# Moving three sets of instructions in a two-layer encoder kernel: third weight sums, differential values, last neighbourhood heads

## The chip, the cores and the metric

The kernel runs on one core of one Trainium2 chip. The metric is the device time of one execution in microseconds; lower is better. The core has engines that each work through their own queue in order: TensorE (PE in the profile; PEld is its weight load), VectorE (DVE), ScalarE (ACT), GpSimd (POOL) and SyncE (SP, which here only issues DMAs). They wait for each other by semaphores.

## The reference

An encoder trunk of two layers over 512 tokens of width 1024, in float32. In each layer three mixers read the same normalised input: differential attention (4 heads of two 64-wide query and key pairs, value width 128), a gated convolution of 31 taps over 512 channels, and neighbourhood attention (8 heads of 64 on a grid of 8 by 64 positions, window 8 by 16, with a bias table per head). Their projections are merged by sigmoid gates, go through an output matrix, then a SwiGLU feed-forward part of width 2816 and a gated per-layer input. A last norm ends it.

```
proj = h @ w_in[i]
qa, ka, va, glu_in, qc, kc, vc, gates = jnp.split(proj, SPLITS, axis=-1)
ya = diff_attention(qa, ka, va, ...)
yb = conformer_conv(glu_in, ...)
yc = neighbourhood_attention(qc, kc, vc, rpb[i])
merged = ga * (ya @ w_br_a[i]) + gb * (yb @ w_br_b[i]) + gc * (yc @ w_br_c[i])
x = x + merged @ w_o[i]
h = rmsnorm(x, norm_ffn[i])
x = x + (jax.nn.silu(h @ w_ffn_gate[i]) * (h @ w_ffn_up[i])) @ w_ffn_down[i]
```

## The kernel before

Channels lie on the 128 partitions and the 512 tokens run along the free axis. Every float32 number that enters a matmul is split into a high half (a ScalarE copy to fp32r) and a low half (a VectorE subtraction, source minus high half), and each product is made of three matmuls: high by high, high by low, low by high (`split`, line 157; `mm3`, lines 177 to 179). So each weight block costs a DMA on SyncE's queue (`weights`, line 171), a copy on ScalarE and a subtraction on VectorE before TensorE can use it. Buffers rotate: 3 for raw weights (`wr`), 3 each for their halves (`wh`, `wl`), 2 for `r` and `kh`, 3 `mm` accumulators in PSUM, 2 `sc`, 2 `tr`, 1 `av`.

TensorE's order is the order of the program text. The other engines are ordered by a scheduler from priorities; weights get a head start (`high_priority`). `behind(i, then)` adds an order between two instructions of the same queue without a semaphore.

Attention units are woven into the projections. `later(gen, delay, gap)` queues a unit; `chunk()` counts blocks of matmuls, every fourth is a tick (`tick`), and at a tick the next due unit emits its next step. In `natten_in(pr, ...)` (phase natten, pr 0 to 3, two heads each) the queries and keys of a pair of heads are projected and split, DMAs stack them (`stack`), and four units (half of the tokens by head, called unit 0 to 3 here) are queued with a delay of 10 ticks for pr 0 and 5 for the others. A unit (`natten_unit`) loads its bias block (`natten_b`, line 675), makes scores (`natten_sc`, line 784), reads them out on VectorE with the bias (line 683), makes exponentials on ScalarE (`natten_e`), takes reciprocals (line 695) and scales; two ticks later TensorE transposes the result (`natten_tr`, lines 707 to 711), it is split (`natten_pt`, `natten_a`); two ticks later it is multiplied by the values (`natten_av` or `natten_mm`, lines 726, 727). The units of pr 3 run while `diff_in(0)`, `diff_v(0)` and `diff_in(1)` project the differential attention.

`diff_v` calls `values` (lines 575 to 603): 512 tokens by 256 value channels in two accumulators of a `mm` buffer each, `accs[0]` for token tiles 0 and 1 and `accs[1]` for 2 and 3. For each of the 8 chunks k of the contraction it does token tiles t = 0 to 3 in turn, three matmuls each (lines 588, 590, 592), with `chunk()` called twice per k. Weights come in two blocks, k = 0 to 3 and k = 4 to 7.

After the mixers, `merge_b` writes the 8 merged chunks (`mergeb_y`, `mergeb_v`: ScalarE copy, VectorE low half), and `w_o` multiplies them by the output matrix, row block after row block, adds the residual, makes the operand of the feed-forward part (`wo_h`) and its sum of squares (`wo_ss`), whose norm follows (`wo_tr`, `wo_sm`, POOL's `wo_rc`, and `wo_tr` again). Along the way `quarters` (lines 911 to 938) makes four combinations of 256-token quarters for each pair of chunks, and splits each: `wo_rp`, `wo_e`, `wo_z`.

The feed-forward part works in 22 blocks fb. Block 0 is done plainly. For all others `seven` (lines 940 to 1018) computes gate and up products of a block by seven products instead of eight, from sums of weight quarters: s1 and s2 are built by loading a block and accumulating another onto it by a DMA from POOL's queue (`ffn_qk<-w_fu`, line 955); s3 = s1 + a22 and s4 = s3 + a12 are two VectorE additions (`ffn_qk<-ffn_qk,ffn_r` and `ffn_qk<-ffn_qk,ffn_wr`), where a22 is a block loaded into an `r` buffer (`ffn_r<-w_fu`, line 953) and a12 is the second half of the block's gate weights. s3 and s4 are then split into `ffn_pt` (odd fb) or `ffn_y` (even fb). TensorE uses them in the sixth and seventh product. The addition s3 is put behind the low half of a22 and, where `first` is set (fb 8, 9, 15 and 16), behind `self.held`, the last low half of an earlier operand.

Of the kernel before, what the change touches and what calls it, by code (L numbers as in the profile page):

```python
# [20 lines left out]
P = 128  # L21
# [5 lines left out]
KD = 8  # L27
# [34 lines left out]
class Net:  # L62
# [512 lines left out]
    def values(self, ap, parts):  # L575


        mm = self.nc.tensor.matmul
        accs = [self.ps("mm", (P, 2, 256)) for _ in range(2)]
        for o in range(0, KD, 4):  # L580
            wh, wl = self.weights(ap[:, o * 256:(o + 4) * 256], 1024)
            for k in range(o, o + 4):
                s = slice((k - o) * 256, (k - o + 1) * 256)
                for t in range(4):
                    out = accs[t // 2][:, t % 2, :]
                    ts = slice(t * P, (t + 1) * P)

                    mm(out, self.h[k][:, 0, ts], wh[:, s], start=k == 0 and t % 2 == 0,
                       stop=False, skip_group_check=True)
                    mm(out, self.h[k][:, 0, ts], wl[:, s], start=False, stop=False,  # L590
                       skip_group_check=True)
                    mm(out, self.h[k][:, 1, ts], wh[:, s], start=False,
                       stop=k == KD - 1 and t % 2 == 1, skip_group_check=True)
                self.chunk()
                self.chunk()
        vs = []
        for acc in accs:
            v = self.sb("v", [P, 2, 512], F32R)
            for t in range(2):
                for hi, lo, a in parts(v[:, t], acc[:, t]):  # L600
                    self.split(hi, lo, a)
            vs.append(v)
        return vs

    def natten_in(self, pr, st, ys):

        self.phase = "natten"
        st4 = self.sb("qk", [P, 4, 512], F32R)
        k2 = self.sb("x", [P, 2, 512], F32R)
        for s, off in enumerate((OFF_QC, OFF_KC)):  # L610
            ps = self.proj(off + pr * P)
            f = 1.0 if s else 0.125
            nat, low = self.sb("kh", [P, 512], F32R), self.sb("t", [P, 512], F32R)
            if pr == 0:

                t = low.bitcast(F32)
                self.stt(t, ps, f, self.rb, ALU.mult, ALU.mult)
                ps, f = t, 1.0
            self.act(nat, ps, AF.Copy, scale=f)
            self.background(self.stt(low, ps, f, nat.bitcast(F32), ALU.mult, ALU.subtract),  # L620
                            self.bg["natten"])
            self.stack(nat, low, st4[:, 2 * s:2 * s + 2], k2 if s else None)
        ys.append(self.sb("y", [P, 2, 512], F32R))
        for n in range(4):
            self.later(self.natten_unit(pr, n // 2, n % 2, st4, k2, st, ys[pr]), 5 if pr else 10, 1)

    def stack(self, nat, low, one, two):

# [282 lines left out]
    def quarters(self, x, h, j):  # L911


        one, two = slice(0, 256), slice(256, 512)
        g = lambda k: self.par(self.i, "ffn", k)
        f = []
        for k in (2 * j, 2 * j + 1):
            v = self.sb("t", [P, 512])
            self.act(v, x[k], AF.Copy, scale=g(k))
            f.append(v)  # L920
        b11, b12, b21, b22 = f[0][:, one], f[0][:, two], f[1][:, one], f[1][:, two]
        u = self.sb("t", [P, 2, 256])
        w = self.sb("t", [P, 2, 256])
        t1, t2, t3, t4 = u[:, 0], u[:, 1], w[:, 0], w[:, 1]
        self.tt(t1, b11, b12, ALU.subtract)
        self.tt(t2, b22, t1, ALU.add)
        self.tt(t3, b22, b12, ALU.subtract)
        self.tt(t4, t2, b21, ALU.subtract)
        if j < 2:
            d = [self.sb("rp" if n < 2 else "e", [P, 2, 256], F32R) for n in range(4)]  # L930
        else:
            d = [q for n in range(2) for q in self.zs[2 * j - 4 + n]]
        for o, t in zip(d, (t1, t2, t3, t4)):
            self.split(o[:, 0], o[:, 1], t)
        ha, hb = self.halves(h[2 * j]), self.halves(h[2 * j + 1])
        cut = lambda p, c: (p[0][:, c], p[1][:, c])
        return dict(b11=cut(ha, one), b21=cut(hb, one), b22=cut(hb, two),
                    **{f"t{n + 1}": (o[:, 0], o[:, 1]) for n, o in enumerate(d)})

    def seven(self, wg, wu, bs, tags, spare, md, first):  # L940


        nc = self.nc
        with self.tc.high_priority(offset=min(self.w_ahead, self.tc.cur_priority - self.p0)):
            lo, up = slice(0, 512), slice(512, 1024)
            g, a22 = self.sb("wr", [P, 1024]), self.sb("r", [P, 512])
            sums = self.sums[self.sevens % 3], self.sums[3]
            self.sevens += 1
            s1, s2, s3, s4 = (s[:, q:q + 512] for s in sums for q in (0, 512))
            nc.sync.dma_start(s1, wg[:, lo])  # L950
            nc.sync.dma_start(s2, wu[:, up])
            nc.sync.dma_start(g, wg)
            nc.sync.dma_start(a22, wu[:, up])
            for q in (s1, s2):
                nc.gpsimd.dma_start(q, wu[:, lo], accum_op=ALU.add)  # L955
            ws = {}

            def halve(hi, lo, src, names):
                i = self.split(hi, lo, src)
                for q, name in enumerate(names):  # L960
                    c = slice(q * 512, q * 512 + 512)
                    ws[name] = (hi[:, c], lo[:, c])
                return i

            wide = lambda: (self.sb("wh", [P, 1024], F32R), self.sb("wl", [P, 1024], F32R))
            halve(*wide(), g, ("a11", "a12"))
            low = halve(self.sb("kh", [P, 512], F32R), self.sb("a", [P, 512], F32R), a22, ("a22",))
            halve(*wide(), sums[0], ("s1", "s2"))
            i = self.tt(s3, s1, a22, ALU.add)
            self.behind(i, low)  # L970
            if first:
                self.behind(i, self.held)
            self.tt(s4, s3, g[:, up], ALU.add)
            halve(*spare, sums[1], ("s3", "s4"))
# [13 lines left out]
        o = self.sb("t", [P, 2, 256])  # L988
# [50 lines left out]
    def ffn(self, h, x):  # L1039
# [7 lines left out]
        for part in PARTS:  # L1047
            mids = []
            for f, fb in enumerate(part):
                tags = (("mm", "mm", "mm"), ("sc", "sc", "av"))[fb % 2]  # L1050
                md = md8[f]
                mids.append(md)
                wg, wu = self.a["w_fg"][i, fb], self.a["w_fu"][i, fb]
                if fb:
                    self.seven(wg, wu, bs, tags, spare[fb % 2], md, part[0] and f < 2)
                    continue
                g = self.sb("t", [P, 512])
                pg, pu = (self.ps(t) for t in tags[:2])
                for j in range(len(QUARTERS), 4):
                    self.four.append(self.quarters(x, h, j))  # L1060
                self.pair((pg, pu), (wg, wu), [h[k] for k in ORDER])

                def gate(pg=pg, g=g):
                    self.tt(g, pg, self.rb, ALU.mult)
                    self.act(g, g, AF.Silu, table="silu")

                self.ready(gate)

                def up(pu=pu, g=g, md=md):
                    self.tt(g, g, pu, ALU.mult)  # L1070
                    self.split(md[:, 0, :], md[:, 1, :], g)

                self.ready(up)
            self.flush()
            down = [self.a["w_fd"][i, m][:, part[0] * P:(part[-1] + 1) * P] for m in range(KD)]
            two = [self.ps(("mm", "sc")[fb % 2 == 0]) for _ in range(2)]
            self.pair(two, down[:2], mids)
            for m in range(KD):
                if m < 2:
                    ps = two[m]  # L1080
                else:
                    ps = self.ps("mm")
                    self.gemm(ps, down[m], mids)
                d = self.sb("t", [P, 512])
                self.tt(d, ps, self.rb, ALU.mult)
                self.tt(x[m], x[m], d, ALU.add)
                if part is PARTS[-1]:
                    if m in (0, 2):
                        qk = self.parts_of("qk", [2, 512], 2, F32R)
                    hn.append(self.norm_chunk(m, x[m], self.par(i, "ple", m),  # L1090
                                              qk[m % 2] if m < 4 else "z", st))
# [315 lines left out]
```

## Time and profile before

| what | value |
|---|---|
| median of 3 runs | 1793.07 us (1792.29 to 1793.09) |
| the profiled execution's own time | 1792.81 us |
| its span from the first to the last instruction | 1791.0 us |
| mean granted TensorE clock | 0.998 |
| PE busy | 1774.5 us (99%) |
| DVE busy | 1410.6 us (79%) |
| ACT busy | 891.6 us (50%) |
| POOL busy | 99.3 us (6%) |
| mean DMA rate | 142 GB/s |

In the rows, a timeline line gives the start in us from the span's start, the duration, engine, source line, operation, output<-inputs by the program's names, shape and count, and in square brackets the idle time of that engine before it and what ended it. A row of waits gives engine, tile and line that waited, whom it waited for, the total in us, how often, and the longest. A row of windows gives a stretch, its length, the busy time of each engine in it with the number of instructions, the granted TensorE clock (1.00 is full), and the DMA share and rate. The whole program is two layers, so a stretch of the first layer comes back 886.9 us later in the second.

### The profile page before, as it was taken

The numbers are of one execution on the slowest core, as the hardware profiler recorded it, in microseconds if no ns is written. First come the engines' busy times: TensorE is split into PE (matmuls) and PEld (weight loads), VectorE is DVE, ScalarE is ACT, GpSimd is POOL, SyncE is SP. The second block draws the span as 40 slices with busy tenths as digits, with TensorE's granted clock in tenths as the row PEclk, the third lists the DMA queues.
The fourth block names the chain that finished last, engine by engine and source line by source line (L and its number), as shares of the span: only waits on it lengthen the run. The fifth ranks groups of instructions, "written<-read, shape, count | busy, mean of one in ns | idle before, by whom it ended". The sixth has DMA issues, their size and how long they took to land.

```text
span 1791.0 us, 27255 instructions
## 1 busy us (share of the span) xinstructions
PE 1774.5 (99%) x10138; PEld 1559.7 (87%) x10138; DVE 1410.6 (79%) x2394; ACT 891.6 (50%) x1551; POOL 99.3 (6%) x142
## 2 busy tenths in 40 slices
PE   9999999999999999999999999999999999999998
PEld 7888888888799899998888888888887998989987
DVE  7877888997788587787776788889887885877776
ACT  5577555325565254454535765552355652534444
POOL 0000000000111011100000000000001110101000
PEclk9999999999999999999999999999999999999999
DMA  5665541334747365544447655422356563746332
GB/s 206 190 182 169 159 124 46 108 98 150 217 130 188 111 166 154 140 123 127 145 125 200 170 161 148 112 71 95 97 182 186 153 173 108 182 133 159 98 103 94
DMA packets 112212, 254.48 MB, mean 142 GB/s; under 512 B 14416, under 2 KB 19024, under 8 KB 112080
## 3 DMA queue, kind: packets, MB, share of 16 engines
q1 hardware_dynamic: 99264, 229.40, 41.9%
q0 software_dynamic: 12096, 22.03, 7.8%
q8 instruction: 80, 1.31, 0.3%
q10 hardware_dynamic: 720, 1.31, 0.2%
q14 instruction: 52, 0.43, 0.1%
HBM read 213.89 MB, written 7.34 MB: 124 GB/s over the span
## 4 chain that ended last, share of the span: by engine, by line
PE 91%; DVE 4%; DMA 2%; ACT 2%; issue 1%; SPq 0%; DVEq 0%; POOLq 0%; ACTq 0%
PE ffn_mm L177 5%; PE ffn_mm L178 5%; PE ffn_mm L179 5%; PE ffn_mm L985 4%; PE ffn_mm L984 4%; PE ffn_mm L983 4%; PE ffn_sc L985 3%; PE ffn_sc L984 3%; PE ffn_sc L983 3%; PE mergea_mm L178 2%; PE mergea_mm L179 2%; PE mergea_mm L177 2%; PE diff_sc L784 2%; PE gatec_mm L177 2%; PE gatec_mm L178 2%; PE gatec_mm L179 2%
## 5 line engine op out<-in xcount | busy, mean ns | idle before, releaser
L160 DVE SCALAR_TENSOR_TENSOR conv_z<-glu_z,pre_par,conv_z 128x512 f32<-128x512 f32 x240 | 179.6, 748 | 3.3
L143 ACT ACTIVATE ffn_wh<-ffn_wr 128x1024 fp32r<-128x1024 f32 (+1 forms) x94 | 94.9, 1015 | 110.0 <-PE ffn_mm L178 75.1
L157 DVE TENSOR_TENSOR ffn_wl<-ffn_wr,ffn_wh 128x1024 fp32r<-128x1024 f32 (+1 forms) x94 | 109.9, 1174 | 5.1 <-ACT ffn_wh L143 4.6
L955 POOL DMA_DIRECT2D ffn_qk<-w_fu x84 | 74.6, 996 | 550.5 <-DMA ffn_qk<-w_fu 218.1
L157 DVE TENSOR_TENSOR ffn_t<-ffn_mm,wo_rb 128x512 f32<-128x512 f32 (+1 forms) x66 | 40.0, 607 | 68.3 <-PE ffn_mm L179 68.3
L143 ACT ACTIVATE mergea_wh<-mergea_wr 128x1024 fp32r<-128x1024 f32 (+1 forms) x32 | 27.1, 846 | 96.8 <-PE mergea_mm L178 79.5
L177 PE MATMUL ffn_mm<-ffn_v,ffn_wh 128*128 128x512 f32 x176 | 68.5, 389 | 0.0
L178 PE MATMUL ffn_mm<-ffn_v,ffn_wh 128*128 128x512 f32 x176 | 68.5, 389 | 0.0
L179 PE MATMUL ffn_mm<-ffn_v,ffn_wl 128*128 128x512 f32 x176 | 68.5, 389 | 0.0
L157 DVE TENSOR_TENSOR ffn_wl<-ffn_qk,ffn_wh 128x1024 fp32r<-128x1024 f32 x42 | 51.4, 1225 | 19.9 <-ACT ffn_wh L143 19.9
L143 ACT ACTIVATE ffn_wh<-ffn_qk 128x1024 fp32r<-128x1024 f32 x42 | 44.5, 1060 | 43.7 <-PE ffn_mm L178 24.5
L157 DVE TENSOR_TENSOR ffn_t<-ffn_t,ffn_t 128x512 f32<-128x512 f32 (+1 forms) x48 | 31.4, 659 | 32.1 <-ACT ffn_t L143 31.5
L143 ACT ACTIVATE diff_a<-diff_sc,diff_s 128x512 f32<-128x512 f32 x32 | 22.0, 687 | 59.0 <-DVE diff_s L875 59.0
L983 PE MATMUL ffn_sc<-wo_h,ffn_wh 128*128 128x256 f32 x176 | 50.0, 284 | 0.0
L985 PE MATMUL ffn_sc<-wo_h,ffn_wl 128*128 128x256 f32 x176 | 49.8, 283 | 0.0
L984 PE MATMUL ffn_sc<-wo_h,ffn_wh 128*128 128x256 f32 x176 | 49.8, 283 | 0.0
L143 ACT ACTIVATE natten_wh<-natten_wr 128x1024 fp32r<-128x1024 f32 x24 | 25.4, 1058 | 41.4 <-issue 15.2
L984 PE MATMUL ffn_mm<-wo_h,ffn_wh 128*128 128x256 f32 x160 | 45.3, 283 | 0.0
L985 PE MATMUL ffn_mm<-wo_h,ffn_wl 128*128 128x256 f32 x160 | 45.3, 283 | 0.0
L983 PE MATMUL ffn_mm<-wo_h,ffn_wh 128*128 128x256 f32 x160 | 45.3, 283 | 0.0
L875 DVE TENSOR_REDUCE diff_s<-diff_sc 128x1 f32<-128x512 f32 x64 | 42.0, 684 | 3.5 <-PE diff_sc L784 3.4
L143 ACT ACTIVATE ffn_kh<-ffn_r 128x512 fp32r<-128x512 f32 x42 | 26.6, 632 | 32.8 <-PE ffn_mm L984 16.2
(825 smaller groups left out, 6577.0 us busy)
## 6 DMA issues: line engine op xcount, KB each, us to landing
ffn_wr<-w_fg SPq DMA_DIRECT2D x44, 512.0 KB, 3.9
ffn_qk<-w_fu POOLq DMA_DIRECT2D x84, 256.0 KB, 5.5
ffn_wr<-w_fd SPq DMA_DIRECT2D x32, 448.0 KB, 3.8
ffn_r<-w_fu SPq DMA_DIRECT2D x42, 256.0 KB, 4.8
ffn_qk<-w_fg SPq DMA_DIRECT2D x42, 256.0 KB, 3.9
ffn_qk<-w_fu SPq DMA_DIRECT2D x42, 256.0 KB, 4.2
natten_wr<-w_in SPq DMA_DIRECT2D x16, 512.0 KB, 4.1
natten_b<-bias SPq DMA_DIRECT2D x32, 256.0 KB, 3.8
```

Of the source, the lines that this page charges most:

```text
L143: i = self.nc.scalar.activation(out, in_, func, **kw)
L157: return self.nc.vector.tensor_tensor(out, a, b, op)
L160: return self.nc.vector.scalar_tensor_tensor(out, a, s, b, op0, op1)
L177: mm(out, wh, ah, start=first, stop=False)
L178: mm(out, wh, al, start=False, stop=False)
L179: mm(out, wl, ah, start=False, stop=last)
L784: self.nc.tensor.matmul(out, st4[:, u, qs], st[:, ks], start=n == 0, stop=n == 1)
L875: nc.vector.tensor_reduce(out=m[:, u:u + 1], in_=sc, op=ALU.max, axis=AX.X, negate=True)
L955: nc.gpsimd.dma_start(q, wu[:, lo], accum_op=ALU.add)
L983: mm(out, wh[:, c], bh, start=first and k == 0, stop=False, skip_group_check=True)
L984: mm(out, wh[:, c], bl, start=False, stop=False, skip_group_check=True)
L985: mm(out, wl[:, c], bh, start=False, stop=k == 3, skip_group_check=True)
```

## The change

Three edits. In `values`, for the first weight block only, the 16 pairs of chunk and token tile are sorted so that all those of `accs[0]` come before those of `accs[1]`; `chunk()` is called after every second pair, as often as before. In `natten_in`, the units of the last pair of heads (pr 3) get a delay of 6 ticks instead of 5. In `quarters`, each split is remembered in `self.held`, and in `seven` the addition s3 of fb 1 and fb 2 is put behind it too.

```diff
@@ values
-            for k in range(o, o + 4):
+            both = [(k, t) for k in range(o, o + 4) for t in range(4)]
+            if o == 0:
+                both.sort(key=lambda kt: kt[1] // 2)
+            for n, (k, t) in enumerate(both):
                 s = slice((k - o) * 256, (k - o + 1) * 256)
-                for t in range(4):
-                    out = accs[t // 2][:, t % 2, :]
...
-                self.chunk()
-                self.chunk()
+                out = accs[t // 2][:, t % 2, :]
...
+                if n % 2:
+                    self.chunk()
@@ natten_in
-            self.later(self.natten_unit(pr, n // 2, n % 2, st4, k2, st, ys[pr]), 5 if pr else 10, 1)
+            self.later(self.natten_unit(pr, n // 2, n % 2, st4, k2, st, ys[pr]), 6 if pr == 3 else 5 if pr else 10, 1)
@@ quarters
         for o, t in zip(d, (t1, t2, t3, t4)):
-            self.split(o[:, 0], o[:, 1], t)
+            self.held = self.split(o[:, 0], o[:, 1], t)
@@ seven
-    def seven(self, wg, wu, bs, tags, spare, md, first):
+    def seven(self, wg, wu, bs, tags, spare, md, first, fb):
...
             i = self.tt(s3, s1, a22, ALU.add)
             self.behind(i, low)
-            if first:
+            if first or fb < 3:
                 self.behind(i, self.held)
@@ ffn
-                    self.seven(wg, wu, bs, tags, spare[fb % 2], md, part[0] and f < 2)
+                    self.seven(wg, wu, bs, tags, spare[fb % 2], md, part[0] and f < 2, fb)
```

What the built programs show: no engine has an instruction more or less. On VectorE, s3 and s4 of fb 1 and the low half of `ffn_pt` move from before the last merged chunk's low half (s3) and from the third set of quarters (s4, `ffn_pt`) to behind the last quarter's low half, where the norm's reduction stands between s3 and s4. On ScalarE the copy of `ffn_pt` moves with them. On SyncE the load of a22 for fb 3, which reuses the `r` buffer that fb 1's s3 reads, moves from between two `wo_x` loads to behind the gate weights of fb 3. fb 2's sums stand where they stood. In the neighbourhood part unit 0 to 3's scores of pr 3 come one tick later on TensorE, and SyncE issues unit 3's bias load behind the eight DMAs that stack the keys of differential head 0, instead of ahead of them. The first accumulation into `accs[1]` comes 18 matmuls later.

More of the change, by code (lines that the diff above doesn't have):

```diff
@@ L581, in values @@
             wh, wl = self.weights(ap[:, o * 256:(o + 4) * 256], 1024)
-            for k in range(o, o + 4):
+            both = [(k, t) for k in range(o, o + 4) for t in range(4)]
+            if o == 0:
+                both.sort(key=lambda kt: kt[1] // 2)
+            for n, (k, t) in enumerate(both):
                 s = slice((k - o) * 256, (k - o + 1) * 256)
-                for t in range(4):
-                    out = accs[t // 2][:, t % 2, :]
[L586 to L593, printed above, removed]
-                self.chunk()
-                self.chunk()
+                out = accs[t // 2][:, t % 2, :]
+                ts = slice(t * P, (t + 1) * P)
+                mm(out, self.h[k][:, 0, ts], wh[:, s], start=k == 0 and t % 2 == 0,
+                   stop=False, skip_group_check=True)
+                mm(out, self.h[k][:, 0, ts], wl[:, s], start=False, stop=False,
+                   skip_group_check=True)
+                mm(out, self.h[k][:, 1, ts], wh[:, s], start=False,
+                   stop=k == KD - 1 and t % 2 == 1, skip_group_check=True)
+                if n % 2:
+                    self.chunk()
         vs = []
```

## The prediction

> **What bounds the kernel now.** I read the page first: TensorE is busy for nearly the whole span, so only its idle time can be won, and each edit is worth what it takes out of TensorE's own waits.
>
> ```profile
> span 1791.0 us, 27255 instructions
> PE 1774.5 (99%) x10138; PEld 1559.7 (87%) x10138; DVE 1410.6 (79%) x2394; ACT 891.6 (50%) x1551; POOL 99.3 (6%) x142
> ```
>
> Idle is 1791.0 - 1774.5 = 16.5 us. The view of TensorE's waits says where:
>
> ```profile
> PE wo_mm L178 <- DVE mergeb_v L157: 6.0, 2, 3.6
> PE natten_tr L709 <- ACT natten_e L143: 0.8, 2, 0.4
> ```
>
> Both come twice, once per layer; the first row is met by the edit of the sums, the second by that of the neighbourhood units; a smaller wait of `diff_mm`, shown below, by that of the values. These rows undercount, since a matmul's shown end lies after the next one's start. So I price a wait by the distance of two starts, less the distance that the same instructions keep undisturbed.
>
> **Edit 1, the third sums.** The timelines of TensorE, VectorE and ScalarE in layer 0:
>
> ```profile
> 463.14 0.39 PE L179 MATMUL wo_mm<-mergeb_v,wo_wl 128*128 128x512 f32 x1
> 463.37 0.39 PE L177 MATMUL wo_mm<-mergeb_v,wo_wh 128*128 128x512 f32 x1
> 467.31 0.50 PE L178 MATMUL wo_mm<-mergeb_v,wo_wh 128*128 128x512 f32 x1 [3.56 <-DVE mergeb_v L157]
> ...
> 465.96 0.69 DVE L157 TENSOR_TENSOR ffn_qk<-ffn_qk,ffn_r 128x512 f32<-128x512 f32 x1 [8.29 <-DMA ffn_qk<-w_fu]
> 466.57 0.69 DVE L157 TENSOR_TENSOR mergeb_v<-gatec_x,mergeb_v 128x512 fp32r<-128x512 f32 x1
> ...
> 457.71 0.63 ACT L143 ACTIVATE mergeb_v<-gatec_x 128x512 fp32r<-128x512 f32 x1 [1.70 <-DVE gatec_x L157]
> ```
>
> VectorE's queue is in order. The s3 of fb 1 stands at its head for 8.29 us, waiting for an accumulating load, and behind it the last merged chunk's low half, whose high half ScalarE had at 458.34. TensorE runs dry. The change puts s3 behind the last quarter's low half; then the low half runs at about 458.4 and is done by 459.1, 4.5 us before TensorE asks (463.60). So the whole wait goes: 467.31 - 463.37 - 0.23 = 3.71 us. Layer 1 has the same wait and something more:
>
> ```profile
> 1350.15 0.39 PE L177 MATMUL wo_mm<-mergeb_v,wo_wh 128*128 128x512 f32 x1
> 1352.99 0.75 PE L178 MATMUL wo_mm<-mergeb_v,wo_wh 128*128 128x512 f32 x1 [2.46 <-DVE mergeb_v L157]
> 1356.52 0.39 PE L177 MATMUL wo_mm<-mergeb_y,wo_wh 128*128 128x512 f32 x1
> ...
> 467.31:470.72 3.41, 3.41 (x15) 2.84 (x16) 2.63 (x4) 2.82 (x4) 1.76 (x2) 1.00 0.90 176
> 1353.00:1356.50 3.50, 3.50 (x8) 2.76 (x9) 1.70 (x3) 2.44 (x3) 1.73 (x2) 0.51 1.09 233
> ```
>
> The wait is 2.84 - 0.23 = 2.61 us, but the next 8 matmuls take 3.53 us where 8 x 0.23 = 1.84 would do: 1.69 more, at a granted clock of 0.51. In layer 0 a longer wait left it at 1.00. The slow stretch goes with its wait, so layer 1 gives 4.30 and both give 8.01 us.
>
> [...]
>
> What is late next? The moved work must still be on time:
>
> ```profile
> 485.10 0.69 DVE L157 TENSOR_TENSOR wo_x<-wo_x,wo_mm 128x512 f32<-128x512 f32 x1 [1.79 <-PE wo_mm L179]
> ...
> 508.09 0.69 DVE L215 TENSOR_REDUCE wo_sm<-wo_tr 128x4 f32<-128x512 f32 x1
> ...
> 509.13 1.03 POOL L222 TENSOR_TENSOR wo_rc<-wo_sm,pre_power 128x4 f32<-128x4 f32 x1 [38.93 <-DVE wo_sm L218]
> ...
> 512.59 0.60 PE L226 MATMUL wo_tr<-pre_ident,wo_rc 128*128 128x128 f32 x4
> ...
> 520.22 0.28 PE L983 MATMUL ffn_sc<-wo_rp,ffn_pt 128*128 128x256 f32 x1
> ...
> L157 DVE TENSOR_TENSOR ffn_wl<-ffn_qk,ffn_wh 128x1024 fp32r<-128x1024 f32 x42 | 51.4, 1225 | 19.9 <-ACT ffn_wh L143 19.9
> ```
>
> VectorE caught up with TensorE at 485.10, so it follows TensorE and moves 3.7 us forward with it. The last quarter's low half ends at about 508.1 - 3.7 = 504.4. Then come, in the built order, s3, the reduction, s4 (each 0.6 from start to start, as 465.96 to 466.57): the norm gains two additions, 1.2 us. The power on POOL then ends at 510.16 - 3.7 + 1.2 = 507.7, and TensorE wants it at 512.59 - 3.7 = 508.9: 1.2 us to spare. `ffn_pt` takes 1.2 us on VectorE by the last row (same shape, 1225 ns) and, taken as long again, on ScalarE before that; s4 ends at 506.2, so it is ready at about 508.7, and wanted at 520.22 - 3.7 = 516.5. Both are hidden; the cover is the 1.2 us. VectorE also sheds s4 and the half of `ffn_pt` from its crowded middle, which I count as nothing. On SyncE the a22 load of fb 3 now waits for s3, at about 505, and the loads behind it with it; they belong to fb 3 and fb 4, which TensorE reaches two and three blocks after fb 1, so not before 516.5. `wo_x` loads, which stood behind that load, come earlier. fb 2's s3 doesn't move: nothing.
>
> **Edit 2, values tile by tile.**
>
> ```profile
> 145.47 0.28 PE L590 MATMUL diff_mm<-diff_wl,glu_h 128*128 128x256 f32 x1
> 145.59 0.28 PE L592 MATMUL diff_mm<-diff_wh,glu_h 128*128 128x256 f32 x1
> 146.16 0.39 PE L588 MATMUL diff_mm<-diff_wh,glu_h 128*128 128x256 f32 x1 [0.29 <-ACT diff_rp L143]
> ```
>
> The first matmul into `accs[1]` waits for ScalarE to empty its PSUM buffer: 0.57 - 0.12 = 0.45 us. With 18 more matmuls of 0.12 us (2.2 us) ahead of it the buffer is long free. Instruction counts stay. On ScalarE the copy of the next key weights now stands ahead of unit 0's exponentials and waits for the last use of the first value weights; the scores come at that time too, so I count nothing. Both layers: 0.90 us.
>
> **Edit 3, units a tick later.** First an undisturbed round of transposes and scores, then the disturbed one; then the same for a later unit:
>
> ```profile
> 156.18 0.28 PE L592 MATMUL diff_mm<-diff_wh,glu_h 128*128 128x256 f32 x1
> 157.32 0.28 PE L588 MATMUL diff_mm<-diff_wh,glu_h 128*128 128x256 f32 x1
> 160.07 0.28 PE L592 MATMUL diff_mm<-diff_wh,glu_h 128*128 128x256 f32 x1
> 162.53 0.40 PE L177 MATMUL diff_mm<-glu_h,diff_wh 128*128 128x512 f32 x1
> 165.80 0.29 PE L707 MATMUL natten_tr<-pre_ident,natten_e 128*128 128x128 f32 x1
> 166.28 0.48 PE L177 MATMUL diff_mm<-glu_h,diff_wh 128*128 128x512 f32 x1
> 169.63 0.29 PE L707 MATMUL natten_tr<-pre_ident,natten_e 128*128 128x128 f32 x1
> 170.56 0.47 PE L177 MATMUL diff_mm<-glu_h,diff_wh 128*128 128x512 f32 x1
> ...
> 159.53 0.16 DVE L695 RECIPROCAL natten_s<-natten_s 128x2 f32<-128x2 f32 x1
> ...
> 156.69 0.33 SPq L675 DMA_DIRECT2D natten_b<-bias  x1
> 160.30 1.14 SPq L633 DMA_DIRECT2D diff_qk<-diff_kh  x2
> 165.25 1.24 SPq L633 DMA_DIRECT2D diff_x<-diff_rp  x2
> ...
> L143 ACT ACTIVATE natten_e<-natten_b,natten_s x10: 494/500/509, 140.1 to 165.5; 128x256 f32<-128x256 f32 x10
> L683 DVE CUSTOM_DVE_ANT_0 natten_b<-natten_sc,natten_b x9: 402/423/425, 140.4 to 163.9; 128x256 f32<-128x256 f32 x9
> ...
> natten_b<-bias SPq DMA_DIRECT2D x32, 256.0 KB, 3.8
> ffn_qk<-w_fu POOLq DMA_DIRECT2D x84, 256.0 KB, 5.5
> ```
>
> Lost now: (2.46 - 1.14) + (0.93 - 0.48) = 1.77 us per layer, the first because unit 1's reciprocal sits at 159.53 behind rotary work on VectorE. One tick later the scores fall among other work: unit 1's normalised values should meet its transposes within 0.1 us. Unit 3 is the worry. Its bias load was issued at 156.69; in the built order it follows the eight stack DMAs (160.30 to 166.49 now; about 1.1 us earlier after, as unit 1's two score reads, 0.42 each, and their hand-overs move from ahead of the rotary work on VectorE to behind it). So it goes out near 165.4 and, with the median 3.8, lands at 169.2. Two score reads, exponential, reciprocal and scaling cost about 2.1 us more (0.42 twice, 0.50, 0.16, 0.50 for the like-shaped scaling, and a hand-over): 171.3. TensorE comes to unit 3's transposes at 169.63 - 0.45 - 1.32 (the waits before it) + 12 x 0.23 (one more block of matmuls) = 170.6. That is 0.7; with hand-overs I take 0.8, and 0.1 for unit 1, and so a gain of 1.77 - 0.9 = 0.87 per layer, 1.7 in both. Bounds: no wait at all gives 3.5; with the 5.5 us of POOL's 256 KB loads the waits are 2.4 + 0.1, which turns the 1.77 into a loss of 0.7, 1.4 in both. I stay near the bias load's own median. Behind unit 3's waiting read on VectorE stand unit 0's and unit 2's results, wanted later.
>
> **Sum.** 8.0 + 0.9 + 1.7 = 10.6 us off 1792.81 (the profiled execution; span 1791.0 plus 1.8 around it), which lies 0.3 below the median of the runs. On the median: 1793.07 - 10.6 = **1782.5**. What a measurement can tell from no change is about 0.2%, 3.6 us.
>
> **Rivals.**
> The half-clock stretch is not in the timed runs: 1.7 less, 1784.2. Against it, the three runs span 0.8 us (1792.29 to 1793.09) and the profiled one, which has it, lies between: 0.08.
> The late units cost as much as I bounded: 1793.07 - 8.9 + 1.4 = 1785.6. For it, the moved bias load: 0.12.
> VectorE, not TensorE, sets the pace up to the norm: its low halves still end at 508.1, the power with two additions ahead at 511.4, and TensorE, there at 508.9 (layer 1: 0.6 earlier), waits 2.5 and 3.1 us: 1782.5 + 5.6 = 1788.1. For it, VectorE's backlog at the end of this stage; against, the 1.79 us idle at 485.10: 0.12.
> The freed time is eaten up there wholly, or the order brings nothing: 1789.5 to 1796.7, taken as 1793: 0.05.
> Slower: unit 3's bias lands so late that VectorE's head blocks and TensorE idles. Each us past 169.2 costs 2 us in the two layers, and a wait over 2.5 us may add the 1.69 of half clock in each. Being 3.6 us slower needs (10.6 + 3.6 - 3.4) / 2 = 5.4 us more, a landing 9.2 us after issue; at 10 us it is 1782.5 + 12.4 + 3.4 = 1798.3. The median of 3.8 speaks against: 0.05.
>
> **Numbers.** The first case keeps 0.58; its own range is 1780.6 (no unit wait) to 1784.8 (edit 3 worth nothing, and 0.6 for a late VectorE). With the half clock and the late units that is 0.78, so the range goes up to VectorE's case: 1780.6 to 1788.1. Faster 0.58 + 0.08 + 0.12 + 0.12 = 0.90, same 0.05, slower 0.05.
>
> **What would show it.** Right: no wait of `wo_mm` for `mergeb_v`, clock 1.00 there in both layers, no wait of the first matmul into `accs[1]`, and at unit 3's transposes a wait under 1 us on `natten_e`. Wrong: TensorE waiting at the second `wo_tr` for `wo_rc`, at `ffn_pt`, or over 2 us in the neighbourhood units; or a `wo_mm` wait that stays.

## The result, and the profile after

The changed kernel takes 1783.11 us (median of 4 runs, 1782.88 to 1783.51); the kernel before, on the same chip, 1793.08 (4 runs, 1792.29 to 1794.02): a ratio of 0.9943, 95% interval 0.9927 to 0.9959. The prediction said 1782.5, in a range of 1780.6 to 1788.1. The profiled execution took 1783.16 us, 9.65 less than that of before (1792.81).

First the head of the page, then the view of TensorE's waits, all that it lists (total, times, longest):

```profile
span 1781.4 us, 27258 instructions
PE 1771.9 (99%) x10138; PEld 1558.2 (87%) x10138; DVE 1410.0 (79%) x2394; ACT 890.6 (50%) x1551; POOL 99.3 (6%) x142
```

```profile
PE pre_av L323 <- DVE pre_zeror L379: 1.1, 1, 1.1
PE natten_tr L712 <- ACT natten_e L143: 0.7, 2, 0.6
PE natten_tr L710 <- ACT natten_e L143: 0.3, 2, 0.2
PE natten_tr L712 <- DVE natten_pt L157: 0.3, 1, 0.3
PE natten_tr L712 <- DVE natten_a L157: 0.2, 1, 0.2
```

The row of `wo_mm` for `mergeb_v` (6.0 us) is gone; what is left belongs to the neighbourhood units and to the start. At the place of the sums, VectorE's timeline in layer 0, then windows of 3.4 us across the former wait in layers 0 and 1 (the columns behind the window are its length, the busy time of each engine, and behind the last brackets TensorE's granted clock, the DMA share and GB/s). In all timelines below, rows that lie between those shown are left out:

```profile
456.95 0.69 DVE L157 TENSOR_TENSOR mergeb_v<-gatec_x,mergeb_v 128x512 fp32r<-128x512 f32 x1 [0.70 <-ACT mergeb_v L143]
462.82 1.37 DVE L157 TENSOR_TENSOR wo_x<-wo_x,wo_mm 128x512 f32<-128x512 f32 x2 [5.18 <-PE wo_mm L179]
```

```profile
462.40:465.80 3.40, 3.40 (x17) 2.81 (x16) 2.98 (x4) 3.16 (x5) 0.90 (x1) 1.00 1.10 286
1345.30:1348.70 3.40, 3.40 (x16) 2.81 (x15) 2.97 (x4) 3.15 (x5) 0.88 (x1) 1.00 1.11 264
```

The low half now starts at 456.95, as soon as ScalarE has the high half, and nothing stands ahead of it. TensorE is busy through both windows, at a granted clock of 1.00.

Where the 9.65 us came from is read by laying the starts of the same TensorE instructions in the two traces side by side, at points between the edits, where the same number of instructions has been issued. The shift grows by these steps: 0.24 at the kernel's start (no edit lies there); layer 0: values 0.61, units 0.54, sums 3.85; layer 1: -0.28 at a unit of an earlier pair of heads (no edit there either), values 0.55, units -0.20, sums 4.37. The rest is within 0.05 a step.

### The profile page after: what moved, and what is told of

The parts are those of the page before. It is cut to its first block, busy times and chain, and to the rows that moved or that the text cites. A ratio compares the mean times of both kernels' runs of the same rounds, so it can differ in the third digit from the quotient of the medians.

```text
span 1781.4 us, 27258 instructions
## 1 busy us (share of the span) xinstructions
PE 1771.9 (99%) x10138; PEld 1558.2 (87%) x10138; DVE 1410.0 (79%) x2394; ACT 890.6 (50%) x1551; POOL 99.3 (6%) x142
## 4 chain that ended last, share of the span: by engine, by line
PE 95%; DVE 2%; ACT 1%; issue 1%; DMA 1%; SPq 0%; DVEq 0%; POOLq 0%; ACTq 0%
PE ffn_mm L177 5%; PE ffn_mm L178 5%; PE ffn_mm L179 5%; PE ffn_mm L988 4%; PE ffn_mm L987 4%; PE ffn_mm L986 4%; PE ffn_sc L988 3%; PE ffn_sc L987 3%; PE ffn_sc L986 3%; PE mergea_mm L177 2%; PE mergea_mm L179 2%; PE mergea_mm L178 2%; PE diff_sc L787 2%; PE gatec_mm L177 2%; PE gatec_mm L178 2%; PE gatec_mm L179 2%
```

## The experiments

The kernel before was timed again beside each group of runs, on four chips (which chip the first runs were made on isn't known here): 1795.57 us (21 runs, 1792.66 to 1797.43) beside the first four kernels, 1794.55 (9) beside the next four, 1795.23 (12) beside the three after them, 1795.11 (13) beside the last. That it is 2 us longer there than in the first runs, and scatters by 5, is a result in itself and comes up below.

**Only the sums.** The changed kernel with the loops of the values and the 5 ticks of before:

```
-            self.split(o[:, 0], o[:, 1], t)
+            self.held = self.split(o[:, 0], o[:, 1], t)
...
-            if first:
+            if first or fb < 3:
```

> Only the third sums are moved; values and units stay as before. My theory, that the parts add up and that the sums bring 3.85 us in layer 0 and 4.37 in layer 1 (the steps between the two traces): 8.2 us, about 1784.9, with no wait of wo_mm for mergeb_v in either layer and clock 1.00 there. Rival A, that the 1.7 us of half clock is a matter of the single execution: 6.4 us, about 1786.7. Rival B, that the sums bring nearly the whole difference of 10 us and the other two edits only shift waits about: about 1783.3.

1784.67 us (1784.31 to 1785.35), ratio 0.9939 (0.9926 to 0.9951). The steps are 3.87 and 4.36, no wait is left there, and the time is as expected. Against the kernel before on the same chip it is 10.9 us, more than the steps of the two first traces give: what the sums remove was larger on this chip. The two traces from it that keep the waits, those of the next two kernels, lose 9.3 and 10.8 us at them, half clock included. One step has no edit beside it: in layer 1 unit 1's transposes start 0.34 us later than in the kernel before, against the matmuls ahead of them (0.35 in the kernel with the sums in layer 0 only, below). Why is open; it blurs every step of the units in layer 1.

**Only the values.** The loops of the first chunks as changed, nothing else.

> Only the values are multiplied tile by tile in the first chunks. My theory: 0.55 us per layer, 1.1 us, about 1792.0, and the first matmul into the second accumulator pair does not wait. The 3.7 and 2.6 us waits of wo_mm stay. Rival: the earlier units meet the same late reciprocal and the wait turns up again there, 1793.1. [...]

1795.83 us (1793.13 to 1797.97), ratio 1.0002 (0.9993 to 1.0011): nothing. The wait for the accumulator pair goes and the shift there is 0.55, but 15 us later it comes back, 0.58 us of it; in layer 1, 0.55 go and 0.55 come back. TensorE, VectorE and ScalarE at unit 1, in this kernel:

```profile
160.10 0.28 PE L595 MATMUL diff_mm<-diff_wh,glu_h 128*128 128x256 f32 x1
160.14 0.16 DVE L698 RECIPROCAL natten_s<-natten_s 128x2 f32<-128x2 f32 x1
160.79 0.89 ACT L143 ACTIVATE natten_e<-natten_e,natten_s 128x256 f32<-128x256 f32 x2
161.34 0.90 PE L712 MATMUL natten_tr<-pre_ident,natten_e 128*128 128x128 f32 x4 [0.95 <-ACT natten_e L143]
```

TensorE arrives earlier at a reciprocal that is as late as ever. The rival was right.

The clock is lost at both waits of `wo_mm` here, at the one of layer 0 too: granted 0.72 in the 3.41 us from the wait's end in layer 0 (466.53) and 0.78 in as long a stretch behind them, 0.63 and 0.87 in layer 1. TensorE's timeline of layer 0 in this kernel:

```profile
463.98 0.39 PE L177 MATMUL wo_mm<-mergeb_v,wo_wh 128*128 128x512 f32 x1
466.53 0.50 PE L178 MATMUL wo_mm<-mergeb_v,wo_wh 128*128 128x512 f32 x1 [2.17 <-DVE mergeb_v L157]
...
467.79 0.39 PE L177 MATMUL wo_mm<-mergeb_y,wo_wh 128*128 128x512 f32 x1
468.02 0.59 PE L178 MATMUL wo_mm<-mergeb_y,wo_wh 128*128 128x512 f32 x1
468.41 0.63 PE L179 MATMUL wo_mm<-mergeb_y,wo_wl 128*128 128x512 f32 x1
```

After the wait the matmuls run at 0.23 us from start to start for 1.5 us, and only then at 0.43: the slow stretch isn't fixed to the end of the wait.

**Only the units.** `6 if pr == 3 else 5 if pr else 10`, nothing else.

> Only the units of the last pair of neighbourhood heads are a stretch later. The prediction's step: 0.87 us per layer, 1.7 us, about 1791.4. What the trace of the changed kernel suggests instead: 0.54 us in layer 0 and a loss of 0.2 in layer 1, so 0.3 us, about 1792.8, with waits left at the transposes of unit 1 (behind the split of the next gate weights) and of unit 3. Rival: alone it brings less still, since the values edit makes room for it: no change or a loss, 1793 to 1794.

1793.76 us (1792.01 to 1794.69), ratio 0.9988 (0.9980 to 0.9997). The steps are 0.57 and 0.59 us, so 1.16 by the trace; by the medians it is 1.8, with an interval of 0.5 to 3.6. By the trace that is more than the trace of the whole change suggested and less than the prediction's 1.74; by the medians it can't be told from 1.74.

**Sums and values, not the units.** The changed kernel with 5 ticks.

> The change without the later units. If the later units bring 0.3 us, this takes about 1783.4; if they bring the 1.7 us of the prediction, 1784.8; if they cost something once the other two edits are there, below 1783.1, down to 1782.5. The waits at the transposes of units 1 and 3 are then as before, 1.3 and 0.45 us.

1785.01 us (1784.57 to 1785.76), ratio 0.9940 (0.9928 to 0.9953), so the values add nothing to the sums (1784.67). Steps of the values and units' stretch: 0.55 won and 0.56 given back in layer 0; in layer 1 0.27 won and 0.71 given back, about half of which the sums alone lose there too. So behind the other two edits the later units are worth 1.9 us by the trace, and 1785.01 - 1783.04 = 2.0 by the medians, the second of these from the next run, on another chip.

**The changed kernel again**, on the chip of the three runs behind it:

> The changed kernel as it is, on the chip of the runs beside it. [...] Rival, that values and units cancel: 1784.7.

1783.04 us (1782.41 to 1783.93), ratio 0.9936 (0.9923 to 0.9950). The rival's 1784.7 did not come: the changed kernel repeats itself in a second set of runs, every execution at a mean clock of 0.999, while the kernel before goes from 1792.90 (0.998) to 1796.25 (0.996).

**Units at 5 ticks, transposes 3 ticks behind the scores.**

```
-        yield 2
+        yield 3 if pr == 3 else 2
         pt = self.ps("tr", (P, 2, 256))
...
-6 if pr == 3 else 5 if pr else 10
+5 if pr else 10
```

> The changed kernel, but the last pair's units start as in the kernel before (5 ticks), and their transposes come 3 ticks after their scores instead of 2. Scores, bias loads, exponentials and the reciprocal then stand where they stood, and only the transposes are one block of 12 matmuls later. My theory, that what is left (0.55 and 0.32 us in layer 0, 1.0 and 0.32 in layer 1) is a reciprocal behind VectorE's splits, expects these waits to go: 2.2 us off 1783.2, about 1781.0. Rival: the exponentials' tiles are held longer and the next unit waits for a free one: 1783 or above.

1785.63 us (1784.90 to 1785.70), 2.6 more than the changed kernel. The waits at unit 1 don't go, they change their reason; the same place in this kernel:

```profile
161.69 1.23 DVE L157 TENSOR_TENSOR gatec_wl<-gatec_wr,gatec_wh 128x1024 fp32r<-128x1024 f32 x1 [0.71 <-ACT gatec_wh L143]
162.67 0.60 ACT L143 ACTIVATE natten_pt<-natten_tr 128x512 fp32r<-128x512 f32 x1
163.30 0.69 DVE L157 TENSOR_TENSOR natten_pt<-natten_tr,natten_pt 128x512 fp32r<-128x512 f32 x1
164.14 0.52 PE L712 MATMUL natten_tr<-pre_ident,natten_e 128*128 128x128 f32 x3 [0.84 <-DVE natten_pt L157]
```

The transposes now wait for the PSUM buffer of the unit ahead, which VectorE empties behind the split of the gate weights and a copy of ScalarE, which ends at 163.27. That is neither of the two reasons given ahead of the run; the rival had the time right and the buffer wrong.

**Units at 6 ticks, transposes 3 behind.** The first hunk alone on the changed kernel.

> The changed kernel with 3 ticks between scores and transposes for the last pair's units, which still start at 6 ticks. The waits at the transposes go as in the run before this one: about 1781.0. Rival: the last unit now ends one block later and its results, or the tiles it holds, come late for the gates behind it: 1783 or above.

1783.37 us (1781.91 to 1784.57), ratio 0.9936 (0.9924 to 0.9948): no different from the changed kernel. The waits of units 1 and 3 are gone in both layers, and later ones have come in the profiled execution, the slowest of the five: 0.84 us at a unit's products in layer 1, 0.42 and 0.70 at the differential scores. Five executions over 2.7 us don't tell whether it is better; by the medians it isn't.

**Units at 7 ticks.**

> The changed kernel with 7 ticks for the last pair's units. Scores, bias loads and transposes move together by another block. My theory, that a unit's wait depends on which split its reciprocal falls behind, and not on having more time: the waits change their size but don't go, 1782.5 to 1784.5. Rival, that the units are simply too early and each further block helps: 1781 to 1782.

1788.35 us (1787.15 to 1789.23), 5.3 more than the changed kernel, beyond what either theory gave. The new stall, once per layer, on VectorE and TensorE in layer 0:

```profile
166.61 1.23 DVE L157 TENSOR_TENSOR diff_wl<-diff_wr,diff_wh 128x1024 fp32r<-128x1024 f32 x1 [1.76 <-ACT diff_wh L143]
167.86 0.42 DVE L686 CUSTOM_DVE_ANT_0 natten_b<-natten_sc,natten_b 128x256 f32<-128x256 f32 x1
168.35 0.39 PE L787 MATMUL natten_sc<-natten_qk 128*128 128x256 f32 x1 [2.10 <-DVE natten_s L686]
```

Unit 2's score read now stands behind a weight split that itself waits 1.76 us, unit 3's scores need the PSUM buffer that the read frees, and TensorE idles 2.1 us.

**The sums in layer 0 only.** `if first or fb < 3 and self.i == 0`, on the kernel with only the sums:

> Only the third sums, and only in layer 0; layer 1 keeps its wait. [...] Rival, that the half clock belongs to this place in layer 1 in every execution: all at 0.998, 1788.6 to 1790.3.

1789.55 us (1788.42 to 1790.63), ratio 0.9971 (0.9960 to 0.9983). The wait of layer 1 is back, as the view of waits has it:

```profile
PE wo_mm L178 <- DVE mergeb_v L157: 3.1, 1, 3.1
```

One wait put back costs 4.9 us by the medians (from 1784.67, on another chip) and 4.88 by the trace, of which the wait itself is 3.25 and half clock behind it about 1.6 (granted 0.53 in the 3.41 us from the wait's end at 1349.95). Five of six executions had a mean clock of 0.998 (1789.36 to 1790.63) and one 0.999, the shortest (1788.42). The rival, that every execution is at 0.998, has that one against it, a single execution.

**The reciprocal first**, on the changed kernel:

```
+        with self.tc.high_priority(offset=20 if pr == 3 else 0):
             nc.vector.reciprocal(m[:, 4:6], m[:, 2:4])
             for t, (_, own) in enumerate(es):
                 self.act(own, own, AF.Copy, scale=m[:, 4 + t:5 + t])
```

> The changed kernel, with a higher priority for the reciprocal and the scaling of the last pair's units, so that unit 1's reciprocal stands ahead of the split of the gate weights on VectorE. My theory, that the wait left at unit 1's transposes (0.55 and 1.0 us) is that split: it goes, and if nothing else turns late the time is about 1.5 us less, 1781.6. Rival: the score read of unit 2 and the rotary work that the new order puts elsewhere are late instead: 1783 or above.

1789.14 us (1787.68 to 1789.89), ratio 0.9967 (0.9955 to 0.9979). Both held in part: the waits at unit 1's transposes are gone, but the new order on VectorE puts rotary work (`diff_rp`) ahead of a score read instead:

```profile
155.61 0.69 DVE L157 TENSOR_TENSOR diff_rp<-diff_rp,diff_rp 128x512 f32<-128x512 f32 x1
156.78 0.42 DVE L686 CUSTOM_DVE_ANT_0 natten_b<-natten_sc,natten_b 128x256 f32<-128x256 f32 x1
157.27 0.39 PE L788 MATMUL natten_sc<-natten_qk 128*128 128x256 f32 x1 [1.95 <-DVE natten_s L686]
```

The edit moves the reciprocal on VectorE and the scaling on ScalarE, so it doesn't tell which of the two queues had held unit 1. And the new wait, 1.95 us with 0.44 more right behind it, is followed by half clock in both layers of the profiled execution, which costs about 1.5 us more each time (granted clock 0.68 and 0.62 in these windows):

```profile
160.68:164.10 3.42, 3.42 (x22) 3.42 (x22) 0.59 (x2) 2.17 (x5) 0.15 (x1) 0.68 0.90 226
1042.68:1046.10 3.42, 2.98 (x13) 2.77 (x14) 1.74 (x8) 2.80 (x9) 0.00 (x0) 0.62 0.67 155
```

**The bias loads earlier.** A higher priority for the last pair's bias loads (`offset=400 if pr == 3 else 100`):

> The changed kernel, with the last pair's bias loads taken ahead of the stack DMAs where the order allows it. In the changed kernel unit 3's bias landed at 168.3, before VectorE was free for its score read (168.9), so my theory expects nothing from the load itself; the new order on VectorE and ScalarE around it may move 1 us either way: 1782 to 1784. Rival, the prediction's, that unit 3's remaining wait is its bias: 0.32 us per layer less, 1782.5.

1789.94 us (1787.88 to 1791.01), ratio 0.9971 (0.9960 to 0.9982), outside what either theory gave. The order around the loads changed as in the run before this one, with nearly the same wait of the scores, 1.96 us at 158.38, and half clock behind it (0.74 granted in the 3.4 us from there, 0.53 in layer 1), so the load's own price was not isolated.

**The kernel before once more**, unchanged:

> The kernel before, unchanged, for another profiled execution. In the first one the wait of 3.7 us in layer 0 kept its clock and that of 2.6 in layer 1 lost it. My theory, that each wait is 2.3 to 3.9 us long, and loses about 1.7 us to half clock or not, by the execution: the mean clock and the time go together again, from 1791.6 at 0.999 or 0.998 to 1797.4 at 0.996, and the profile shows a half-clock stretch behind neither, one or both waits, with a time to match. Rival, that the clock belongs to the place: layer 0 at clock 1.00 and layer 1 near 0.51 again.

1795.12 us (10 runs, 1791.79 to 1796.90). TensorE in layer 0 and layer 1 of its profiled execution:

```profile
466.98 0.50 PE L178 MATMUL wo_mm<-mergeb_v,wo_wh 128*128 128x512 f32 x1 [2.61 <-DVE mergeb_v L157]
...
1353.51 0.79 PE L178 MATMUL wo_mm<-mergeb_v,wo_wh 128*128 128x512 f32 x1 [3.25 <-DVE mergeb_v L157]
1354.10 0.63 PE L179 MATMUL wo_mm<-mergeb_v,wo_wl 128*128 128x512 f32 x1
```

The waits are 2.77 and 3.41 us here (3.71 and 2.61 in the first execution). The clock is again kept in layer 0 (granted 1.00 in both stretches of 3.41 us behind the wait) and lost in layer 1 (0.50, then 0.60), this time for 14 matmuls and 2.9 us, where the first execution lost it for 8 and 1.7. Two executions alone would fit the rival, that the clock belongs to the place. The same wait in the kernels with only the values and only the units speaks against it: layer 0 lost its clock in both (granted 0.72 and 0.59 in the first such stretch).

## Why the prediction was right, and where its terms were off

**The sums, 8.0 predicted, 8.22 measured.** 3.71 and 4.30 against steps of 3.85 and 4.37. The cause is shown by the two kernels that have the sums alone, in both layers or in one: the wait goes where the addition is behind the low half and stays where it is not. That the size fits so closely is partly luck: the trace that priced the term is also the one from which the steps are measured, and beside the kernel with the sums alone the executions of the kernel before lost 10.9 us.

**The cover of the sums held, and was larger than worked out.** VectorE and the engines behind it at the entry of the feed-forward, layer 0:

```profile
502.39 0.69 DVE L157 TENSOR_TENSOR ffn_qk<-ffn_qk,ffn_r 128x512 f32<-128x512 f32 x1
502.99 0.69 DVE L215 TENSOR_REDUCE wo_sm<-wo_tr 128x4 f32<-128x512 f32 x1
503.59 0.69 DVE L157 TENSOR_TENSOR ffn_qk<-ffn_qk,ffn_wr 128x512 f32<-128x512 f32 x1
504.44 1.03 POOL L222 TENSOR_TENSOR wo_rc<-wo_sm,pre_power 128x4 f32<-128x4 f32 x1 [35.14 <-DVE wo_sm L218]
505.40 1.22 DVE L157 TENSOR_TENSOR ffn_pt<-ffn_qk,ffn_pt 128x1024 fp32r<-128x1024 f32 x1 [1.04 <-ACT ffn_pt L143]
507.32 0.60 PE L226 MATMUL wo_tr<-pre_ident,wo_rc 128*128 128x128 f32 x4
514.94 0.28 PE L986 MATMUL ffn_sc<-wo_rp,ffn_pt 128*128 128x256 f32 x1
```

The order is the one foreseen: s3, the reduction, s4. The power ends at 505.47 and is asked for at 507.32, 1.85 us to spare (1.2 predicted); `ffn_pt` is ready at 506.6 and wanted at 514.94, 8.3 us later (7.8 predicted). The rival in which VectorE sets the pace falls with these rows: it did move forward with TensorE. On SyncE the a22 load of fb 3 went out at 503.11 (about 505, less the 1.4 us by which TensorE was earlier, was predicted), and no wait of TensorE follows from it.

**Values and units, 2.6 predicted, 1.5 measured.** The step that was off is the price of each of the two: both were worked out as if TensorE met nothing behind them that was late as well. The values' 0.90 fails first: TensorE meets their wait and unit 1's one behind the other, and with only the values the 0.45 that the prediction booked was given back 15 us later (0.58). In layer 0 it stays once the units are later: the pair brought 0.61 + 0.54 = 1.15 us, the units alone 0.57, where 0.45 + 0.87 = 1.32 was predicted. In layer 1 the pair brought 0.35 and the units alone 0.59, so there it isn't shown to stay.

Three sizes inside the pair were off. Unit 1 was to wait 0.1 and waits 0.63 in layer 0 and 1.02 in layer 1: from the last matmul ahead of its transposes to the first one behind the scores TensorE takes 1.88 and 2.27 us, where the same instructions take 1.25 in the kernel with 6 and 3 ticks. The place in the changed kernel, layer 0:

```profile
160.05 1.22 DVE L157 TENSOR_TENSOR gatec_wl<-gatec_wr,gatec_wh 128x1024 fp32r<-128x1024 f32 x1
160.53 0.60 ACT L143 ACTIVATE natten_pt<-natten_tr 128x512 fp32r<-128x512 f32 x1
161.20 0.16 DVE L698 RECIPROCAL natten_s<-natten_s 128x2 f32<-128x2 f32 x1
161.45 0.51 ACT L143 ACTIVATE natten_e<-natten_b,natten_s 128x256 f32<-128x256 f32 x1
161.96 0.89 ACT L143 ACTIVATE natten_e<-natten_e,natten_s 128x256 f32<-128x256 f32 x2
162.51 0.90 PE L712 MATMUL natten_tr<-pre_ident,natten_e 128*128 128x128 f32 x4 [0.17 <-ACT natten_e L143]
```

One tick later the reciprocal has left the rotary work and come behind the split of the next gate weights, 1.22 us, which the prediction didn't look for. But it is done at 161.36, and the scaling that the transposes need starts only at 161.96, when ScalarE is through with copies of unit 0's results and an exponential of unit 2. ScalarE shows no idle time there, so in this order its queue ended last, not the split; no run here separates the two. (The bracket shows 0.17 because a matmul's shown end is late: those ahead of it are shown 0.39 us long and start 0.23 apart. The starts are 0.33 us further apart than undisturbed, with 0.30 more inside the transposes.)

In layer 1 unit 0's transposes and the scores behind them take 1.51 us by the same measure, 0.37 more than in layer 0. The prediction had no wait there. Here it is a reciprocal behind rotary work again, which itself waited for a DMA:

```profile
1037.93 0.69 DVE L157 TENSOR_TENSOR diff_rp<-diff_rp,diff_r 128x512 f32<-128x512 f32 x1 [0.76 <-DMA diff_rp<-diff_rp]
...
1039.81 0.16 DVE L698 RECIPROCAL natten_s<-natten_s 128x2 f32<-128x2 f32 x1
1040.00 0.91 ACT L143 ACTIVATE natten_e<-natten_e,natten_s 128x256 f32<-128x256 f32 x2 [2.64 <-DVE natten_s L698]
1040.56 0.90 PE L712 MATMUL natten_tr<-pre_ident,natten_e 128*128 128x128 f32 x4
```

Unit 3 was to wait 0.8 for its bias and waits 0.46 in both layers, as much as before (0.45), 0.32 of it ahead of the transposes:

```profile
165.37 0.53 SPq L678 DMA_DIRECT2D natten_b<-bias  x1
...
167.66 1.23 DVE L157 TENSOR_TENSOR diff_wl<-diff_wr,diff_wh 128x1024 fp32r<-128x1024 f32 x1 [0.76 <-ACT diff_wh L143]
168.92 0.42 DVE L686 CUSTOM_DVE_ANT_0 natten_b<-natten_sc,natten_b 128x256 f32<-128x256 f32 x1
...
171.29 0.33 PE L710 MATMUL natten_tr<-pre_ident,natten_e 128*128 128x128 f32 x1 [0.16 <-ACT natten_e L143]
```

The load went out at 165.37 (165.4 predicted) and took 2.9 us instead of the median 3.8, so it landed at 168.3, before VectorE was done with a split at 168.9. The bias didn't set that wait; a split did. So the rival of late units (1785.6) falls on its own ground: unit 3 cost less than was taken, and what was lost was lost at unit 1 and, in layer 1, at unit 0.

**The half clock** was in the rivals with the wrong sign. The prediction feared that the timed runs might lack it (1784.2, 0.08). The later executions have it more often than the profiled one: of the nine waits of `wo_mm` that the five traces with this wait show, six lost 1.5 to 1.7 us to half clock behind them, a seventh 2.9 and two nothing, and beside the experiments 55 of 65 executions of the kernel before had a mean clock of 0.996 or 0.997, where the changed kernel has 0.999. Of these 65, the 33 at 0.996 have a median of 1795.9 us, the 22 at 0.997 1794.2, the 8 at 0.998 1794.6, the 2 at 0.999 1793.0: clock and time go together, though not in every step, since the waits themselves vary, from 2.32 us (only the values, layer 0) to 3.71 (the first execution of before, layer 0) in the rows shown. With these waits goes their scatter, and so the same change is worth 10.0 us beside the first runs of before and 11.5 beside those of the second set.

**Slower** (1798.3) did not come, but its kind is real: one tick more than the change's 6 costs 5.3 us. There the read of the scores blocks, behind a split, and not the landing of the bias.

## What to carry to other kernels

The wait of s3 at the head of VectorE's queue (8.29 us idle in layer 0) was worth here the whole wait of TensorE behind it and the half clock that followed it in layer 1 (steps of 3.85 and 4.37 us); look for what stands behind such a wait that someone needs sooner, and let that go ahead. Small waits that one engine meets one after the other were not to be added up here (of the values' 0.55 us, 0.58 came back 15 us later): remove the first, and ask at what time the engine then reaches the second. When a step is moved by a slot, list what the other engines have in their queues at the new place, on VectorE the weight splits of 1.2 us and the rotary work of 0.7, on ScalarE the copies of 0.6 and the exponentials of 0.5, since here nearly every placement of the units that was run traded one such wait for another.

## What the runs showed of the hardware

The length of an idle stretch didn't tell whether the clock would fall, and 2.5 us, which the slower case of the prediction names, didn't divide them. Idle TensorE stretches at `wo_mm` of 2.17 us (only the values, layer 0), 2.46 and 3.25 (the kernel before, layer 1 of its first and second execution) and 3.10 (the sums in layer 0 only, layer 1) were followed by half clock: granted 0.72, 0.51, 0.50 and 0.53 in the 3.41 us behind them, with 0.43 us from one matmul's start to the next in the slow part instead of 0.23. So were the other waits of these kinds (only the values, layer 1: 0.63; only the units: 0.59 and 0.56), and the idle stretches of 1.95 and 1.96 us in both layers of the profiled executions with the reciprocal first (0.82, then 0.68, in layer 0, 0.62 in layer 1) and with the earlier bias loads (0.74 and 0.53). Those of 2.61 and 3.56 at `wo_mm` (the kernel before, layer 0), and of 2.10 in both layers of the profiled execution at 7 ticks, were not: 1.00 in as long a stretch behind each. Waits at the units of up to 0.84 us idle left a mean clock of 0.999 or 1.000 in all 19 executions of the three kernels whose profiled executions show no longer one there (the changed kernel, in both its sets, and those of 5 and 3 and of 6 and 3 ticks). Other executions with the waits of 1.95 and 1.96 were at 0.997 to 0.999, with 2.10 at 0.998 or 0.999.

Half clock began with the matmul behind the wait (1353.51 in the second execution of the kernel before) or later: with only the values 1.5 us later, at 468.02, and with the reciprocal first mostly in the second of two such stretches behind the wait of layer 0 (0.68 against 0.82 in the first). It lasted 3.5 us, 8 matmuls, in layer 1 of the first execution of the kernel before, and 6.1 us, 14 matmuls, in that of the second. Why one wait kept the clock and another lost it, no run here shows.
